# A hybrid decoder layer with 32 streamed experts: gate units among the projections, later MLA norms, other places for output weights and biases

## The chip, the core and the metric

The kernel runs on one core of a Trainium2 chip. TensorE (PE) multiplies matrices, VectorE (DVE) and ScalarE (ACT) do elementwise work, GpSimd (POOL) helps with it, and SyncE (SP) issues the transfers, which run on 16 DMA engines. The metric is device microseconds from the start to the end of one execution; less is better. Three runs of the kernel before took 1162.37, 1165.75 and 1166.36 us, a median of 1165.75.

## What is computed

One decoder layer on 256 tokens of width 1024, in float32. The reference, cut to its frame:

```python
proj = rmsnorm(x, g_mix) @ w_in          # q, k, v | c_q, c_kv, k_pe | gate_a, gate_b
q_a = apply_rope(rmsnorm(q_a, moba_q_norm)); k_a = apply_rope(rmsnorm(k_a, moba_k_norm))
y_a = moba_attention(q_a, k_a, v_a)      # 8 heads of 64; one block of 256: causal softmax
q_b = rmsnorm(c_q, mla_q_lat_norm) @ w_uq;  kv = rmsnorm(c_kv, mla_kv_lat_norm) @ w_ukv
...                                      # norm and rope of q_b, k_b (8 heads of 96)
y_b = causal_attention(q_b, k_b, v_b)
merged = sigmoid(gate_a) * (y_a @ w_branch_a) + sigmoid(gate_b) * (y_b @ w_branch_b)
x = x + merged @ w_out
x = x + routed_experts(rmsnorm(x, g_ffn), ...)   # top 4 of 32, clamped SwiGLU, 1024 wide
x = x + sigmoid(rmsnorm(x, g_ple) @ w_ple_gate) * (p_i @ w_ple_proj)
```

## The kernel before

The program has two parts. The first, up to about 215 us, is all that stands ahead of the experts; the second is a loop, written out, over 32 experts, and a short tail for the last gate.

**Weights of the first part** come as units of 128x1024 float32 (512 KB), in the order of the list `KINDS`: latent projection (a), q, k, the up projections (u), v, 16 gate units (g), 8 branch units (b) and 8 output units (o). `fetch` issues their loads on SyncE into four places `raw` (ring slot 6) and three places `raw_x`; `raw_of` gives the place, and from unit `RAW_LAST` on only the three `raw_x` are used. `make_unit` splits a unit in two fp32r halves: ACT casts the high half (L210), DVE subtracts 5/8 of the low half and GpSimd 3/8 (both L214); for output units DVE subtracts all. `unit` does that up to three units ahead of the one that PE takes. Each product is then three matmuls, high by high, high by low and low by high (`three`, L251 to L253).

**The order** in the first part: latent and q projections, `moba_norm(0)` (norm and rotation of q, with the multiplies by the norm's factor at L358), k projection, `moba_norm(1)`, up projections, v projection, one gate unit, transposes (`moba_T`), `mla_norm` (statistics, the factor chain called hb, rotation, and the multiplies of q by hb at L470), another gate unit. Then eight steps of attention, each with the scores of the next pair of heads, a gate unit, the probabilities' transposes (PT, L550), another gate unit and the values. In `scores` the fixed factor 1/sqrt(d) is applied with the mask (L534). After the attention come the branch products with the merge by gates, and the output projection (wo) in two halves of 512 columns; the router's transposes and logits lie between its units. Engines run their instructions in order; the code's order and the scheduler of the framework set it.

**Expert weights** are pieces of 2 MB, four for gate and up and two for down per expert, listed in `seq`. They go into ten slots: 0 to 7 of the ring, and 8 and 9, which exist once the pool of gates is closed. `release` issues the next piece on SyncE into a slot that has been given free in the program. Ahead of the loop the slots serve other ends and are given up one after another: 7 after the first projection, 3 after the k projection, 6 once unit `RAW_LAST` is made, 5 after the first attention half, 4 after the attention, then 8, 9, and 0 to 2 after the output projection. The gates are kept in three tiles of a pool of their own (`t8`), the three-fold expert biases in the tile `pre8`, which are loaded after the attention and split into bf16 parts (L661 to L667).

**The loop**: gather by a one-hot product (L779), gate and up product (L818), SwiGLU on DVE and ACT, transposes, down product (L842) and scatter into accumulators (L852). At expert 20 stands a branch (`overflow`, L898): if any expert has more than 64 tokens, an inner loop loads its weights again. With these inputs the branch is not taken. `load` issues on SyncE unless another engine is named.

## Time and profile before

| | |
|---|---|
| median of three runs | 1165.75 us |
| the profiled execution | 1165.23 us |
| its span, first to last instruction | 1163.5 us |
| PE busy | 1076.0 us (92%) |
| DVE, ACT, POOL busy | 337.9, 201.4, 78.2 us |
| moved by DMA | 440.18 MB, mean 378 GB/s over the span |

The rows below are numbered in groups. Times are us from the span's start, unless marked ns. A name such as L818 is a line of the kernel; "g<-w_g,xg" says what is written from what. "A <- B" in a list of waits says that A sat idle until B ended. A Q behind an engine's name (SPq, PEq) is its instruction queue. PEclk is the clock that TensorE was granted, as a share of full speed.

### The profile page before, as it was taken

How to read it: one execution, taken by the hardware profiler on the slowest of the kernel's cores; microseconds unless marked ns; L12 is line 12 of the kernel's file. 1: busy time of each engine (PE TensorE's matmuls, PEld its weight loads, DVE VectorE, ACT ScalarE, POOL GpSimd, SP SyncE). 2: the span in 40 equal slices, each digit the busy share in tenths (PEclk: the TensorE clock that was granted, in tenths of full speed). 3: DMA queues.
4: the chain of work that ended last, by engine and by line, in shares of the span. 5: the costliest groups of instructions: out<-in, count | busy, mean ns of one | idle time of the engine just before them, and what ended most of it. 6: DMA issues, size and time to landing. Idle time of an engine off the chain costs nothing. (4 is left out here: it accounts for less than half of the span.)

```text
span 1163.5 us, 13110 instructions
## 1 busy us (share of the span) xinstructions
PE 1076.0 (92%) x5446; PEld 525.8 (45%) x5446; DVE 337.9 (29%) x754; ACT 201.4 (17%) x375; POOL 78.2 (7%) x84
## 2 busy tenths in 40 slices
PE   8889999999999999998889999998899999998988
PEld 6668997543434343343333434333334333333336
DVE  6987686321111122111110111120111111111136
ACT  5547644211000000000001000000000000000024
POOL 5553320000000000000000000000000000000000
PEclk9999999999999999999999999999999999999999
DMA  9653568699999999999999999999899999999991
GB/s 363 221 181 113 184 225 317 274 430 430 429 431 430 431 430 431 429 429 409 432 431 430 430 430 430 431 431 426 347 432 430 430 430 431 430 430 431 427 412 40
DMA packets 39649, 440.18 MB, mean 378 GB/s; under 512 B 4384, under 2 KB 5152, under 8 KB 14144
## 3 DMA queue, kind: packets, MB, share of 16 engines
q1 hardware_dynamic: 39584, 439.27, 90.7%
q8 instruction: 45, 0.74, 0.2%
q14 instruction: 20, 0.16, 0.0%
HBM read 438.21 MB, written 1.05 MB: 378 GB/s over the span
## 5 line engine op out<-in xcount | busy, mean ns | idle before, releaser
L818 PE MATMUL g<-w_g,xg 128*64 128x512 f32 x1024 | 295.4, 597 | 28.3 <-DMA w_g<-in_wgu 24.3
L818 PE MATMUL u<-w_g,xg 128*64 128x512 f32 x1024 | 292.5, 593 | 0.0
L842 PE MATMUL y<-w_d,ht 128*64 128x512 f32 x1024 | 234.5, 596 | 14.5 <-DMA w_d<-in_wdn 12.9
L822 DVE TENSOR_SCALAR g<-g 128x512 f32<-128x512 f32 x32 | 22.1, 691 | 467.2 <-PE g L812 467.2
L818 PEld LDWEIGHTS g<-w_g,xg 128*64 128x64 f32 x1024 | 79.3, 136 | 172.4 <-issue 120.6
L818 PEld LDWEIGHTS u<-w_g,xg 128*64 128x64 f32 x1024 | 83.1, 137 | 144.7 <-issue 141.9
L842 PEld LDWEIGHTS y<-w_d,ht 128*64 128x64 f32 x1024 | 72.8, 136 | 139.4 <-issue 119.3
L824 ACT ACTIVATE th<-g 128x512 f32<-128x512 f32 x32 | 20.2, 630 | 482.9 <-DVE g L822 482.9
L847 DVE COPY ys<-y 64x512 f32<-64x512 f32 x32 | 22.2, 695 | 171.2 <-ACT ys L846 171.1
L852 PE MATMUL acc<-ys,owT 128*128 128x512 f32 x128 | 59.2, 605 | 8.8 <-ACT ys L846 8.8
L846 ACT COPY ys<-y 64x512 f32<-64x512 f32 x32 | 18.5, 579 | 262.0 <-PE y L842 262.0
L852 PEld LDWEIGHTS acc<-ys,owT 128*128 128x128 f32 x128 | 22.9, 189 | 45.7 <-ACT ys L846 21.1
L779 PE MATMUL g<-oh,h_perm 128*128 128x128 f32 x256 | 33.1, 282 | 6.8 <-DVE g L822 5.6
L210 ACT CAST fr<-raw_x 128x1024 fp32r<-128x1024 f32 (+1 forms) x33 | 33.9, 1033 | 21.8 <-PE proj L253 5.6
L214 POOL TENSOR_TENSOR fr<-raw_x,fr 128x384 fp32r<-128x384 f32 (+1 forms) x25 | 34.6, 1389 | 44.9 <-ACT fr L210 37.9
L779 PEld LDWEIGHTS g<-oh,h_perm 128*128 128x128 f32 x256 | 29.9, 191 | 16.9 <-DVE g L822 10.6
L214 DVE TENSOR_TENSOR fr<-raw_x,fr 128x640 fp32r<-128x640 f32 (+2 forms) x33 | 33.0, 1000 | 5.8 <-ACT fr L210 5.6
L779 PEld LDWEIGHTS u<-oh,h_perm 128*128 128x128 f32 x256 | 29.8, 192 | 8.1 <-issue 8.1
L252 PE MATMUL proj<-fr,fr 128*128 128x512 f32 (+1 forms) x64 | 26.0, 406 | 7.1 <-DVE fr L214 6.5
L779 PE MATMUL u<-oh,h_perm 128*128 128x128 f32 x256 | 32.2, 279 | 0.0
L251 PE MATMUL gate<-fr,fr 128*128 128x256 f32 x104 | 31.2, 300 | 0.0
L253 PE MATMUL gate<-fr,fr 128*128 128x256 f32 x104 | 30.1, 290 | 0.0
(316 smaller groups left out, 1124.5 us busy)
## 6 DMA issues: line engine op xcount, KB each, us to landing
w_g<-in_wgu SPq DMA_DIRECT2D x124, 2048.0 KB, 32.1
w_d<-in_wdn SPq DMA_DIRECT2D x62, 2048.0 KB, 32.9
raw_x<-in_wpre SPq DMA_DIRECT2D x38, 512.0 KB, 4.3
w_g<-in_wgu SPq DMA_DIRECT2D x8, 1024.0 KB, 28.6
raw<-in_wpre SPq DMA_DIRECT2D x8, 512.0 KB, 6.2
w_d<-in_wdn SPq DMA_DIRECT2D x4, 1024.0 KB, 24.5
w_ple<-in_w_ple_gate SPq DMA_DIRECT2D x8, 512.0 KB, 14.1
raw<-in_wpre SPq DMA_DIRECT2D x4, 416.0 KB, 7.6
```

Source lines behind the costliest of these rows:

```text
L210: A.copy(hi, src)
L214: e.tensor_tensor(lo[:, a:b], src[:, a:b], hi[:, a:b], op=ALU.subtract)
L251: T.matmul(o, lh, rh, start=first, stop=False)
L252: T.matmul(o, lh, rl, start=False, stop=False)
L253: T.matmul(o, ll, rh, start=False, stop=last)
L779: T.matmul(b[:, k * P:(k + 1) * P], h_perm[:, tt, (half * 4 + k) * P:(half * 4 + k + 1) * P], oh[:, tt], start=(tt == 0), stop=(tt == 1))
L818: T.matmul(gu[i][half * CAP:(half + 1) * CAP], xg[:, k], wv_, start=(k == 0), stop=False)
L822: V.tensor_scalar_min(g, gu[0], 7.0)
L824: A.activation(th, g, AF.Tanh, scale=0.851)
L842: T.matmul(y[g * CAP:(g + 1) * CAP], ht[:, f % 4, (f // 4) * CAP:(f // 4 + 1) * CAP], w[:, dh * 512:(dh + 1) * 512], start=(f == 0), stop= ...
L847: V.tensor_copy(ys[CAP:P, 1 - odd], y[CAP:P])
L852: T.matmul(acc[tt][dh], owT[:, dh, tok(tt)], ys[:, dh], start=first, stop=last)
```

## The change

- `KINDS` puts one gate unit behind each of the q, k and v projections, and the v projection ahead of the up projections; the other 13 gate units follow. The gates are kept in ring slot 3, which no longer takes a piece after the k projection. Four gate units now stand ahead of the first scores, one in each attention step up to the fifth ahead of the transposes, and one behind them in seven steps.
- The factor of q's norm, times 1/sqrt(d), is no longer multiplied into q but given to the exponential as its scale, and to the maximum; that takes away the two multiplies at L358 for q and those at L470. `moba_norm` and the transposes of the latents stand behind the v projection. `mla_norm` is cut in `mla_stats` (behind the second scores) and `mla_norm` (behind the third).
- The first four output units have places of their own in slot 4 after the attention (`raw_o`); slot 4 takes its piece when the fourth is made. Slot 6 takes its piece at unit 24 instead of 18.
- The biases are loaded into slot 3 after the merge, and split in the code where they were; slot 3 takes its piece behind the split. The additional tile for split units is there before the first scores.
- The loads of the overflow loop are issued by GpSimd.

```diff
--- before.py
+++ after.py
@@ -46,14 +46,14 @@
 C_ALL = 1859


-KINDS = (("a", 4, 832), ("q", 4, 1024), ("k", 4, 1024), ("u", 1, 1024), ("u", 1, 512), ("u", 1, 1024), ("v", 4, 1024),
-         ("g", 16, 1024), ("b", 8, 1024), ("o", 8, 1024))
+KINDS = (("a", 4, 832), ("q", 4, 1024), ("g", 1, 1024), ("k", 4, 1024), ("g", 1, 1024), ("v", 4, 1024), ("g", 1, 1024),
+         ("u", 1, 1024), ("u", 1, 512), ("u", 1, 1024), ("g", 13, 1024), ("b", 8, 1024), ("o", 8, 1024))
 UNITS = [(kind, n) for kind, c, n in KINDS for _ in range(c)]
 U_OFF = [sum(n for _, n in UNITS[:i]) for i in range(len(UNITS) + 1)]

-N_RAW, N_EXTRA, RAW_LAST = 4, 3, 18
+N_RAW, N_EXTRA, RAW_LAST = 4, 3, 24
 FIRST_O = len(UNITS) - 8
-LAST_THREE = 27
+LAST_THREE = 25

 WARM0, WARM2, WARM3, WARM5 = 30, 30, 8, 10
 AHEAD = 3
@@ -180,6 +180,8 @@
     made, used, sent_units, holder = [0], [0], [0], {}

     def raw_of(n):
+        if FIRST_O <= n < FIRST_O + N_RAW:
+            return N_RAW + N_EXTRA + n - FIRST_O, raw_o[0][:, n - FIRST_O]
         i = n % (N_RAW + N_EXTRA) if n <= RAW_LAST else N_RAW + n % N_EXTRA
         t = raw[:, i] if i < N_RAW else raw_x[:, i - N_RAW]
         return i, t[:, 0:UNITS[n][1]]
@@ -194,6 +196,8 @@

         while sent_units[0] < limit:
             n = sent_units[0]
+            if n >= FIRST_O and not raw_o:
+                return
             i, t = raw_of(n)
             if holder.get(i, -1) >= made[0]:
                 return
@@ -201,7 +205,7 @@
             load(t, wpre[:, U_OFF[n]:U_OFF[n + 1]])
             sent_units[0] += 1

-    taken = {}
+    taken, raw_o = {}, []

     def make_unit(n):
         src = raw_of(n)[1]
@@ -225,6 +229,8 @@
             made[0] += 1
             if m == RAW_LAST:
                 release(6)
+            if m == FIRST_O + N_RAW - 1:
+                release(4)
             fetch()
         return (split[split_of(n)][:, u, 0:UNITS[n][1]].rearrange("p (k f) -> p k f", k=k) for u in range(2))

...
+    both_gates = slot(3, "sg")
+    sg = [both_gates[:, o:o + 2048].rearrange("p (u t) -> p u t", u=8) for o in (0, 2048)]
+    gi = iter(range(16))
+    def gate_unit():
+        a, ft = divmod(next(gi), 8)
+        b = bank("gate")
+        wh, wl = unit(8)
+        for k in range(8):
+            three([(b[:, :S], (wh[:, k], wl[:, k]), (xh[:, k], xl[:, k]))], k == 0, k == 7)
+        o = sg[a][:, ft, :]
+        V.tensor_tensor(o, b[:, :S], rbc, op=ALU.mult)
+        A.activation(o, o, AF.Tanh, scale=0.5)

     project(512, lambda tt, b: A.mul(qk[:, tt, 0:512], b, xrs[:, tt:tt + 1]))
+    rbw = wk.tile([P, 2, P], F32, name="rbw")
+    rbc = wk.tile([P, S], F32, name="rbc")
+    for tt in range(2):
+        V.tensor_scalar_mul(rbw[:, tt], ones, xrs[:, tt:tt + 1])
+    b = bank("rbc")
+    for tt in range(2):
+        T.matmul(b[:, tok(tt)], rbw[:, tt], ident, start=True, stop=True)
+    V.tensor_copy(rbc, b[:, :S])
+    gate_unit()
+    project(512, lambda tt, b: A.mul(qk[:, tt, 512:1024], b, xrs[:, tt:tt + 1]))

     G.tensor_tensor(w_r, w_r, gkp.unsqueeze(2).broadcast_to([P, 8, NE]), op=ALU.mult)
     kpe = wk.tile([P, 2, 32], F32, name="kpe")
...
+    gate_unit()
+    project(512, lambda tt, b: A.mul(va[:, tt], b, xrs[:, tt:tt + 1]))
...
-    b = bank("rbc")
-    for tt in range(2):
-        T.matmul(b[:, tok(tt)], rbw[:, tt], ident, start=True, stop=True)
-    V.tensor_copy(rbc, b[:, :S])
-    project(512, lambda tt, b: A.mul(qk[:, tt, 512:1024], b, xrs[:, tt:tt + 1]))
-    release(3)
-    moba_norm(1)
+    gate_unit()
+    qscale = [None, None]
...
+        hrs = rsqrt(wk, hss.rearrange("p a b -> p (a b)"), 16, 64, f"ha{i}")
+        if not i:
+            V.tensor_scalar_mul(hrs, hrs, 64.0 ** -0.5)
+            qscale[0] = hrs.rearrange("p (t h) -> p t h", t=2)
...
+            if i:
+                V.tensor_tensor(src, src, hrs[:, tt].unsqueeze(2).broadcast_to([P, 8, 64]), op=ALU.mult)
+    moba_norm(0)
...
-    project(512, lambda tt, b: A.mul(va[:, tt], b, xrs[:, tt:tt + 1]))
+    moba_norm(1)
+    gate_unit()
...
-    def mla_norm():
+    brs = [None]
+    def mla_stats():
...
-        brs = rsqrt(wk, bss.rearrange("p a b -> p (a b)"), 32, 96, "hb")
-        brs = brs.rearrange("p (t h) -> p t h", t=2)
+        r = rsqrt(wk, bss.rearrange("p a b -> p (a b)"), 32, 96, "hb").rearrange("p (t h) -> p t h", t=2)
+        V.tensor_scalar_mul(r[:, :, 0:8], r[:, :, 0:8], 96.0 ** -0.5)
+        qscale[1] = r[:, :, 0:8]
+        brs[0] = r
+    def mla_norm():
...
-            V.tensor_tensor(q4[:, tt], q4[:, tt], brs[:, tt, 0:8].unsqueeze(2).broadcast_to([P, 8, 96]), op=ALU.mult)
-            kr = brs[:, tt, 8:16].unsqueeze(2)
+            kr = brs[0][:, tt, 8:16].unsqueeze(2)
...
-        scale = (96.0 if mla else 64.0) ** -0.5
+        scale = qscale[int(mla)]
...
+                V.tensor_tensor_reduce(pr[:, c0:c1], b[:, c0:c1], mask[:, c0:c1], 1.0, NEG, ALU.add, ALU.max,
                                        mx[:, i:i + 1])
-            V.tensor_scalar_mul(mx[:, 2:4], mx[:, 0:2], -1.0)
+            h = 2 * j + u
+            V.scalar_tensor_tensor(mx[:, 2:4], in0=mx[:, 0:2], scalar=-1.0, in1=scale[:, :, h], op0=ALU.mult, op1=ALU.mult)
...
-                A.activation(pr[:, c0:c1], pr[:, c0:c1], AF.Exp, bias=mx[:, 2 + i:3 + i], accum_out=mx[:, 4 + i:5 + i])
+                A.activation(pr[:, c0:c1], pr[:, c0:c1], AF.Exp, bias=mx[:, 2 + i:3 + i], scale=scale[:, i, h:h + 1],
+                             accum_out=mx[:, 4 + i:5 + i])
...
-    sg.append(t8tile("sga"))
-    gi = iter(range(16))
-    gate_unit(next(gi))
     moba_T()
-    mla_norm()
-    gate_unit(next(gi))
+    split.append(t8tile("split").bitcast(FR))
     Ps = {0: scores(0, False)}
     for j in range(8):
         if j + 1 < 8:
             Ps[j + 1] = scores((j + 1) % 4, j + 1 >= 4)
-        if j < 7:
-            gate_unit(next(gi))
+        if j == 0:
+            mla_stats()
+        if j == 1:
+            mla_norm()
+        if j < 5:
+            gate_unit()
         pts = probs_T(Ps.pop(j))
         if j < 7:
-            gate_unit(next(gi))
+            gate_unit()
         values(j % 4, j >= 4, pts)
         if j == 3:
             release(5)
@@ -587,17 +617,12 @@
             for i in range(2):
                 mla_T(i, 0)
                 mla_T(i, 1)
-            sg.append(t8tile("sgb"))
-            split.append(t8tile("split").bitcast(FR))
     att_stack.close()
-    b96 = h8[0:96]
-    load(b96, bgu3)
     mixed = gate_stack.enter_context(tc.tile_pool(name="mixed", bufs=2, side="right"))
-    release(4)
...
-    sga = sg[0].rearrange("p t (u f) -> p (t u) f", u=4)
-    sgb = sg[1].rearrange("p t (u f) -> p (t u) f", u=4)
+    raw_o.append(slot(4, "raw_o").rearrange("p (n f) -> p n f", n=N_RAW))
...
+    sga, sgb = sg
...
     gate_stack.close()
+    b96 = slot(3, "b96")[0:96, 0:2048]
+    load(b96, bgu3)
...
         V.tensor_copy(bgu[r, c], b96[r, c])
+    release(3)
...
                     for k in range(8):
-                        load(wt, wgu[bass.ds(e, 1), k // 2, :, k % 2 * 2048:k % 2 * 2048 + 2048].rearrange("o p f -> p (o f)"))
+                        load(wt, wgu[bass.ds(e, 1), k // 2, :, k % 2 * 2048:k % 2 * 2048 + 2048].rearrange("o p f -> p (o f)"), G)
                         gate_up_k(gu, xg, k, wt)
...
                     for f in range(8):
-                        load(wt[:, 0:1024], wdn[bass.ds(e, 1), f // 4, :, f % 4 * 1024:f % 4 * 1024 + 1024].rearrange("o p f -> p (o f)"))
+                        load(wt[:, 0:1024], wdn[bass.ds(e, 1), f // 4, :, f % 4 * 1024:f % 4 * 1024 + 1024].rearrange("o p f -> p (o f)"), G)
                         down_k(y, ht, f, wt[:, 0:1024], 0)
...
```

SyncE, the issues around the merge: raw_x and raw_o are units, w_gCE and w_dCE piece C of expert E, b96 and pre8 the biases. Before:

```order
L80 DMA w_g01_1646<-in_wgu 128x4096
L80 DMA raw_x_85<-in_wpre 128x1024 x9
L80 DMA w_g11_1982<-in_wgu 128x4096
L80 DMA raw_x_85<-in_wpre 128x1024
L80 DMA w_g21_2013<-in_wgu 128x4096
L80 DMA w_d10_2105<-in_wdn 128x4096
L80 DMA w_g31_2101<-in_wgu 128x4096
L80 DMA w_d00_2103<-in_wdn 128x4096
```

Now:

```order
L80 DMA raw_x_85<-in_wpre 128x1024 x4
L80 DMA b96_1939<-in_bgu3 96x2048
L80 DMA w_g30_1965<-in_wgu 128x4096
L80 DMA w_g01_1979<-in_wgu 128x4096
L80 DMA raw_x_85<-in_wpre 128x1024
L80 DMA w_g11_2010<-in_wgu 128x4096
L80 DMA w_d00_2102<-in_wdn 128x4096
L80 DMA w_g21_2098<-in_wgu 128x4096
L80 DMA w_g31_2100<-in_wgu 128x4096
L80 DMA w_d10_2131<-in_wdn 128x4096
```

Before, the biases and the pieces g30 and g01 were sent ahead of the merge's end and five pieces behind it; now the biases stand ahead of seven pieces.

DVE around the first scores: L534 and L562 are the masked scores with their maximum, hb_ the factor chain of the MLA norm, L501 and L364 gates, L214 and L218 unit splits. Before:

```order
L501 TENSOR_TENSOR sga<-gate,rbc 128x256
L456 TENSOR_SCALAR bss<-bss,kps 128x8
L214 TENSOR_TENSOR fr_81<-raw_x,fr_81 128x640
L88 TENSOR_SCALAR hb_m<-bss 128x32
L534 ISA pr,mx<-S,mask 128x128
L534 ISA mx 128x1
L90 TENSOR_SCALAR hb_s<-hb_m 128x32
L534 ISA pr,mx<-S,mask 128x256
L534 ISA mx 128x1
L92 TENSOR_SCALAR hb_r<-hb_s 128x32
```

Now:

```order
L218 TENSOR_TENSOR fr_80<-raw,fr_80 128x640
L490 TENSOR_REDUCE bss<-pre_64 128x8
L364 TENSOR_TENSOR sg<-gate,rbc 128x256
L492 TENSOR_REDUCE bss<-kbf 128x8 x2
L494 TENSOR_SCALAR bss<-bss,kps 128x8 x2
L510 TENSOR_TENSOR qb<-qb,pre_64 128x768
L511 TENSOR_TENSOR qb<-qb,rt_778 128x8x32
L490 TENSOR_REDUCE bss<-pre_64 128x8
L562 ISA pr,mx<-S,mask 128x128
L562 ISA mx 128x1
```

The hb chain has left the first scores; split units and gates stand ahead of them in its place.

DVE in the output projection: xs<-wo is a half's residual, 128x1024 from raw_x an output unit's split, bgu and pre8 or b_1939 the biases. Before, from the last bias operations on:

```order
L666 TENSOR_TENSOR pre_64<-pre_64,bgu 32x512
L214 TENSOR_TENSOR fr_81<-raw_x,fr_81 128x1024
L667 CAST bgu<-pre_64 32x512
L214 TENSOR_TENSOR fr_80<-raw_x,fr_80 128x1024
L652 SCALAR_TENSOR_TENSOR xs<-wo,xs 128x512 x2
L214 TENSOR_TENSOR fr_80<-raw_x,fr_80 128x1024
L652 SCALAR_TENSOR_TENSOR xs<-wo,xs 128x512 x2
```

Now, from the first half's residual on, the start and the end of the stretch:

```order
L218 TENSOR_TENSOR fr_80<-raw_x,fr_80 128x1024
L679 SCALAR_TENSOR_TENSOR xs<-wo,xs 128x512 x2
L693 TENSOR_TENSOR b_1939<-b_1939,bgu 32x512
L689 TENSOR_TENSOR b_1939<-b_1939,bgu 96x512
L694 CAST bgu<-b_1939 32x512
L690 CAST bgu<-b_1939 32x512
L692 CAST bgu<-b_1939 32x512
```

```order
L692 CAST bgu<-b_1939 32x512
L693 TENSOR_TENSOR b_1939<-b_1939,bgu 32x512
L694 CAST bgu<-b_1939 32x512
L218 TENSOR_TENSOR fr_80<-raw_x,fr_80 128x1024
L679 SCALAR_TENSOR_TENSOR xs<-wo,xs 128x512 x2
L699 TENSOR_TENSOR fss<-fss 128x2
```

Between the first half's residual and the last unit's split now stand 19 bias operations; before there were none.

## Rows read from the trace of the kernel before

**Rows 1.** Chain of waits: start us, us, what; two pieces before TensorE's tail.

```profile
1046.94 40.00 DMA w_d<-in_wdn
1086.98 3.65 PE y L842 x16
```

**Rows 2.** Timeline of SyncE's queue: start us, us, line; the first issue in the loop.

```profile
222.78 0.33 SPq L80 DMA_DIRECT2D w_g<-in_wgu  x1
```

**Rows 3.** Windows, loop: stretch, us, busy (instructions) by engine, PEclk, DMA share, GB/s.

```profile
215.40:222.80 7.40, 7.40 (x50) 4.83 (x52) 3.72 (x13) 0.00 (x0) 0.00 (x0) 1.00 0.26 113
222.80:816.00 593.20, 565.80 (x2690) 221.85 (x2688) 98.78 (x192) 45.46 (x80) 0.00 (x0) 1.00 1.01 428
816.00:828.00 12.00, 12.00 (x75) 6.82 (x73) 4.13 (x8) 1.56 (x3) 0.00 (x0) 1.00 0.61 233
828.00:1133.00 305.00, 272.55 (x1272) 104.58 (x1268) 47.94 (x85) 24.90 (x40) 0.00 (x0) 1.00 1.01 429
```

**Rows 4.** TensorE's waits: who waits <- for whom: us in total, times, longest.

```profile
PE g L818 <- DMA w_g<-in_wgu: 24.3, 21, 2.3
PE y L842 <- DMA w_d<-in_wdn: 12.9, 17, 1.3
...
PE proj L252 <- DVE fr L214: 6.5, 5, 2.2
...
PE PT L550 <- DVE hb_r L97: 4.8, 2, 4.4
```

**Rows 5.** Timeline of TensorE: a gate unit's first, the next operation, the loop's first.

```profile
71.42 0.28 PE L251 MATMUL gate<-fr,fr 128*128 128x256 f32 x1
...
74.30 0.93 PE L436 MATMUL qkT<-cst,qk 128*128 128x128 f32 x7
...
215.35 2.02 PE L779 MATMUL g<-oh,h_perm 128*128 128x128 f32 x16 [1.20 <-issue]
```

**Rows 6.** Waits of SyncE's queue: the overflow branch.

```profile
SPq L898 <- SPq L898: 29.5, 2, 24.7
```

**Rows 7.** Line L898 on SyncE: ns min/median/max, first and last start us.

```profile
L898 SPq EVENT_SEMAPHORE  x8: 17/17/17, 818.1 to 823.4; - x8
...
L898 SPq COMPARE_BRANCH  x1: 50/50/50, 793.4 to 793.4; - x1
```

**Rows 8.** Windows, DVE's tight stretch: sum of 14:35, 35:50, 50:71, 71:88.

```profile
sum 74.00, PE 62.21 PEld 50.57 DVE 66.25 ACT 39.19 POOL 45.42; mean PE 15.55 PEld 12.64 DVE 16.56 ACT 9.80 POOL 11.35
```

**Rows 9.** DVE by line and form, 0 to 240 us: busy us, mean ns | idle before.

```profile
L214 DVE TENSOR_TENSOR fr<-raw_x,fr 128x640 fp32r<-128x640 f32 x24 | 22.7, 948 | 1.5 <-ACT fr L210 1.3
...
L356 DVE TENSOR_TENSOR qk<-qk,pre 128x512 f32<-128x512 f32 x4 | 5.5, 1366 | 1.4 <-POOL pre L354 1.4
...
L501 DVE TENSOR_TENSOR sga<-gate,rbc 128x256 f32<-128x256 f32 x8 | 3.3, 416 | 1.7 <-PE gate L253 1.7
...
L666 DVE TENSOR_TENSOR pre<-pre,bgu 32x512 f32<-32x512 f32 x4 | 3.3, 813 | 0.1
...
L358 DVE TENSOR_TENSOR qk<-qk,ha_r 128x512 f32<-128x512 f32 x4 | 2.6, 685 | 0.0
...
L470 DVE TENSOR_TENSOR qb<-qb,hb_r 128x768 f32<-128x768 f32 x2 | 1.9, 945 | 0.0
...
L665 DVE CAST bgu<-pre 32x512 bf16<-32x512 f32 x4 | 1.7, 418 | 0.1
```

**Rows 10.** Windows before the loop, columns as in rows 3.

```profile
35.00:50.30 15.30, 13.06 (x51) 9.84 (x51) 14.50 (x31) 3.92 (x6) 7.42 (x8) 0.89 0.44 138
79.00:88.30 9.30, 4.90 (x41) 4.11 (x40) 9.30 (x33) 4.66 (x14) 6.65 (x5) 1.00 0.40 115
88.30:111.40 23.10, 22.73 (x179) 20.42 (x179) 18.88 (x69) 14.90 (x44) 7.76 (x4) 0.93 0.33 95
177.70:205.60 27.90, 26.68 (x122) 21.79 (x121) 16.38 (x26) 10.35 (x16) 0.00 (x0) 0.94 0.85 323
```

**Rows 11.** Page, DMA issues: transfer, queue, count, KB each, us to landing.

```profile
w_g<-in_wgu SPq DMA_DIRECT2D x124, 2048.0 KB, 32.1
```

54 lines of the change are left out of this document (19 added, 35 removed).

## The prediction, made before the result

> **What bounds the kernel now.** I read the chain of waits first. Backwards from the end it is TensorE (PE) for some 76 us, and before 1086.98 it is one expert-weight transfer after another [rows 1]. The windows say the same of the rate: from the first loop transfer at 222.78 [rows 2] to 816 the core moves 428 GB/s and from 828 on 429 GB/s with the DMA share at 1.01, and PE is busy only 565.8 of 593.2 us in the first of these stretches [rows 3]. The list of PE's waits agrees: 24.3 us in 21 waits for gate-up weights and 12.9 us in 17 for down weights [rows 4]. So the loop from 222.8 to 1087 runs at the rate of the weight stream, and PE has 37.2 us to spare in it. Nothing in the change makes the stream itself smaller; only two things can shorten the time: the stream resumes earlier, or it has fewer holes.
>
> Two holes show. From 215.4 to 222.8 the rate is 113 GB/s: all ten slots hold pieces and the next transfer leaves only when the first gate-up piece has been used up [rows 2, 3]. PE begins the loop's first gather at 215.35 [rows 5]; the first slot comes free 7.4 us later. So whatever brings PE to that gather earlier brings the rest of the stream, and with it the end, earlier by as much, as long as the slots are full by then. The second hole is 816 to 828, at 233 GB/s [rows 3]. There SyncE stands 24.7 us in the branch around the overflow loop: the branch is reached at 793.4, and eight semaphore waits follow from 818.1 to 823.4 [rows 6, 7].
>
> **The change, part by part.** The sum is made against the profiled execution's 1165.23 us (span 1163.5 and 1.7 around it); the median of the runs shown is 1165.75, 0.5 us more, which I leave out.
>
> 1. *Overflow loads by GpSimd.* In the branch that is not taken, SyncE's eight waits are for the counts of its own loads in that loop. SyncE issues the weight stream too, so it stands until pieces that it sent before the branch have landed, and sends none meanwhile. With the loads on GpSimd the not-taken side has its waits on GpSimd, which has no loads under way and nothing later to do for SyncE; SyncE goes on after a few branch instructions. Refund: (430 − 233) GB/s × 12 us = 2.36 MB, at 430 GB/s 5.5 us. PE waits 37.2 us for the stream in all, so the refund reaches the end. Ends: 0 if another wait keeps SyncE there, 5.5 if none does; I take 5.5, since the rows name SyncE's own queue as releaser. The additional semaphore waits at the kernel's end cost some tenths; I take 0.
>
> 2. *Projections up to the first probabilities.* Here VectorE (DVE) is the tight engine: 66.25 us busy of the 74 us from 14 to 88, while PE is busy 62.21 [rows 8]. PE waits 6.5 us for weight splits by DVE in the projections, and 4.8 us for the chain of the MLA factor (hb), which stands in the middle of the first scores' softmax [rows 4]. The change drops the multiplies of q by its factor: two at L358, 0.685 each, and two at L470, 0.945 each, together 3.3 us [rows 9]. It puts the hb chain and one of the two rotations of the MLA q behind the first probabilities. By the order that is some dozen operations, most of them smaller than any row here or only trading places with the scores' own; I count four at the 0.42 us of the cheapest row, 1.7 us. It adds two gate units ahead of the first scores (four before the first score matmul instead of two, and one more behind): two splits of 0.95 and two evacuations of 0.42, 2.7 us [rows 9]. DVE then has 66.25 − 3.3 − 1.7 + 2.7 = 64.0 us; at the same share of 0.895 that takes 71.5 us instead of 74: 2.5 us earlier. The other end is PE's: its idle time in the stretch is 74 − 62.2 = 11.8 us, and the two additional units fill 5.8 of it, so at most 6.0 us. I take 3.5, nearer to the DVE end, because DVE was the fuller engine. On top, two more gate units are then done that before came later, and PE is the limit there (busy 22.73 of 23.1 us, then nearly all of it [rows 10]). One unit takes PE 71.42 to 74.30 = 2.88 us [rows 5], so 5.8 us. Together **9.3**, between 8.3 and 11.8 if the order does what it says; less is the first rival.
>
> 3. *Clock.* In the K projection the granted clock is 0.89 over 15.3 us, and after the wait for hb 0.93 over 23.1 us [rows 10]; that is 1.7 + 1.6 us of missing clock, each behind a stretch in which PE waited (79 to 88.3 it was busy 4.9 of 9.3 us). A gate unit between projections gives PE work while DVE splits. I take 1.0; ends 0 and 3.3.
>
> 4. *Output weights, biases.* From 177.7 to 205.6 PE is busy 26.68 of 27.9 us at clock 0.94 [rows 10]: 1.2 idle and 1.7 lost to the clock, 2.9 at most to win. The last output unit waits for its transfer before; now four units have their own places and come earlier. Against it, 19 of the 24 bias operations now stand on DVE between the two halves of the output projection, ahead of the last unit's split (the order below the change). At 0.42 to 0.81 us each [rows 9] that is 8 to 15 us. They start after the first half, about 15 of the 27.9 us into the stage, and PE asks for that unit, the last of eight, some 22 us in. The low end costs PE about 2 us, the high end 9. The higher means come from operations slowed beside GpSimd, which has no instruction in this stage [rows 10], so I take near the low end, and a gain of **1.5** for the whole part from the 2.9 less its share; ends −5 and 2.9.
>
> 5. *Places.* Two weight pieces more than before have to be fetched after the merge, because slots 3 and 4 are lent to gates, output units and biases: 2 × 2.1 MB [rows 11] at 430 GB/s = 9.8 us, less about 1.5 for output units fetched earlier. Idle transfer time there before: 27.9 × (1 − 323/430) = 6.9 us, and 7.4 × (1 − 113/430) = 5.5 us in the hole [rows 3, 10], so 12.4 against 8.3. It fits with some 4 us left. I take 0; the third rival is that it doesn't.
>
> Sum: 5.5 + 9.3 + 1.0 + 1.5 = 17.3 us, 1165.2 − 17.3 = 1147.9, so **1148**. PE's slack of 37.2 us carries it: after the 5.5 some 32 us of waiting for weights are left, and a start moved as a whole takes none of it.
>
> **Rivals.** *A: DVE stays the bound and the projections give little.* For it: DVE operations beside GpSimd are long; the rotation's multiply at L356 takes 1.37 us where L358 with the same 128x512 takes 0.685 [rows 9], and GpSimd's share of each split stays. If the two units only push DVE's work later, part 2 gives nothing beyond 2 to 5 us and part 4 nothing: from 1165.2 − 5.5 = 1159.7 down to 1153.5. Against it: the gate units' PE work has to be done anyway and idle PE time of 11.8 us lies ahead of it. The Trainium skill speaks for it ("SBUF — State Buffer", "Who interferes with whom"): a DVE instruction with two SBUF inputs contends with a GpSimd instruction that reads SBUF. By that rule each unit moved into this stretch puts one more GpSimd subtract beside the rotations; the rows of L356 and L358 agree with it in size.
>
> *B: the loads by GpSimd change nothing.* The hole would stay if SyncE waited there for something other than its own loads: 1165.2 − 11.8 = 1153.4. The Trainium skill ("DMA: Bandwidth & Descriptors", "Issuing engines are not separate DMA queues") says that transfers from any engine end on the same 16 engines and that another issuer saves only issue time. By that rule alone a new issuer would give nothing. The rows show 24.7 us of SyncE waiting, not issuing, so I give it little.
>
> *C, slower: the store is not full when the loop begins.* Seven pieces are sent after the merge, where five were. They leave SyncE in one order, behind one load for biases that needs its slot from the gates, and one output unit's place. If the first leaves as late as the end of the output projection, all seven (14.7 MB, 34 us) land some 62 us after the merge where the first release came 45 us after it (222.8 − 177.7): 17 us of stream lost. With nothing gained in the projections that gives 1165.2 − 5.5 + 17 = 1176.7. It decides from the point where the first piece leaves more than about 6 us after the merge. Against it: the slot of the first piece is empty at the merge's end, and only the queue stands before it.
>
> **How the numbers follow.** Forecast 1148, with 1142 to 1153 as its own range: 0.68. A 0.16 (1153 to 1160), B 0.05, C 0.04, and 0.07 for more than forecast (parts 2 to 4 near their upper ends, down to 1137). The range 1141 to 1156.5 leaves out C, the worse half of A and the best of the last. A measurement can tell about 0.5%, 5.8 us: faster means below 1159.9. The forecast, B, most of A and the better side give 0.90 for that; the worst of A and mild forms of C 0.06 for the same; C 0.04 for slower.
>
> **What would show it.** In the profile of the changed kernel: no wait of SyncE in the overflow branch and 430 GB/s from 816 to 828's counterpart; the first gather of the loop about 12 us earlier, near 203.5; PE's wait for splits in the projections below 6.5 us and none for hb ahead of the first probabilities; the stage of the output projection near 26.4 us; and the rate between first gather and first release still low, as a sign that the slots were full. The prediction is wrong if the first gather is less than 5 us earlier, if PE waits for weights within the first expert, or if the branch still stops SyncE.

## The result and the profile after

Measured on one chip with the kernel before, four runs each: **1156.55 us** (1154.64 to 1156.99) against 1165.42 us (1162.37 to 1166.36). The ratio is 0.9915, 95% interval 0.9894 to 0.9935: a gain of 8.9 us by the medians and 9.9 by the ratio, about half of the 17.3 forecast. The time lies outside the forecast's own 1142 to 1153, among those of rival A, and at the upper edge of the whole range, 1156.5. The profiled execution took 1156.99 us with a span of 1155.3.

I first laid the places side by side that the prediction names, by the start of TensorE's (PE's) first operation in each:

```
us from the span's start              before    after   earlier   predicted
first probabilities transposed (PT)    88.34    93.25    -4.91      +3.5
merge done, output projection begins  177.71   172.43     5.28     +10.3
loop's first gather                   215.35   210.58     4.77     +11.8
first slot released                   222.78   218.01     4.77     +11.8
last wait for a weight piece ends    1086.98  1078.57     8.41     +17.3
```

So in this pair of profiles 4.8 us came from the stages before the loop, where I wanted 11.8, and 3.6 us from inside the loop, where I wanted 5.5. The prediction named three signs of being wrong. One has come: the first gather is less than 5 us earlier. The other two have not: PE waits for no weights within the first expert, and the branch no longer stops SyncE.

Windows of the changed kernel (columns as in [rows 3]): its tight stretch of projections, the 23.1 us behind the first probabilities, the output projection, first gather to first release, and three around the overflow branch.

```profile
71.00:93.00 22.00, 18.13 (x116) 15.71 (x114) 15.04 (x37) 15.63 (x30) 11.79 (x12) 0.92 0.36 133
...
93.20:116.30 23.10, 22.98 (x195) 20.77 (x196) 21.04 (x78) 17.51 (x46) 6.68 (x5) 1.00 0.37 115
...
172.40:200.80 28.40, 25.97 (x123) 21.01 (x122) 22.60 (x38) 8.99 (x15) 0.00 (x0) 0.96 0.87 342
...
210.60:218.00 7.40, 7.40 (x50) 4.86 (x52) 3.75 (x13) 0.00 (x0) 0.00 (x0) 1.00 0.94 403
...
780.00:800.00 20.00, 13.96 (x56) 5.28 (x54) 4.10 (x9) 2.27 (x4) 0.00 (x0) 0.90 1.01 424
800.00:812.00 12.00, 12.00 (x52) 4.19 (x50) 0.00 (x0) 0.00 (x0) 0.00 (x0) 0.89 1.01 429
812.00:830.00 18.00, 18.00 (x104) 8.89 (x102) 5.15 (x9) 1.79 (x3) 0.00 (x0) 1.00 1.01 431
```

The hole of 233 GB/s at the branch [rows 3] is gone. The output projection takes 28.4 us, no shorter than in [rows 10], where 26.4 was forecast. The rate between first gather and first release is 403 GB/s where it was 113 and was to stay low: pieces were still landing there, so the slots were filled only just in time.

PE's waits in the changed kernel (who waits <- for whom: us in total, times, longest), against [rows 4]:

```profile
PE g L846 <- DMA w_g<-in_wgu: 18.0, 17, 2.3
PE y L870 <- DMA w_d<-in_wdn: 10.1, 14, 1.4
...
PE g L846 <- PEq L926: 5.4, 1, 5.4
PE proj L258 <- DVE fr L218: 4.8, 4, 1.9
PE PT L580 <- DVE pr L571: 2.4, 1, 2.4
PE wo L258 <- DVE fr L218: 2.4, 1, 2.4
```

The wait for hb ahead of the probabilities has gone, as predicted, and two new ones of 2.4 us have come: one ahead of the same transposes, and one in the output projection. 28.1 us of waiting for weights remain, so the loop is still bound by the stream.

### The profile page after: what moved, and what is told of

Read it like the earlier page. It is cut to its first block, busy times and chain, and to the rows that moved or that the text cites. A ratio compares the mean times of both kernels' runs of the same rounds, so it can differ in the third digit from the quotient of the medians.

```text
span 1155.3 us, 13098 instructions
## 1 busy us (share of the span) xinstructions
PE 1076.9 (93%) x5446; PEld 525.8 (46%) x5446; DVE 337.2 (29%) x752; ACT 205.3 (18%) x375; POOL 75.1 (7%) x84
## 5 line engine op out<-in xcount | busy, mean ns | idle before, releaser
L218 POOL TENSOR_TENSOR fr<-raw_x,fr 128x384 fp32r<-128x384 f32 (+1 forms) x21 | 27.3, 1305 | 40.6 <-ACT fr L214 39.2
L819 DVE TENSOR_SCALAR ow<-oh,whalf 128x128 f32<-128x128 f32 x64 | 14.0, 282 | 54.6 <-PE owT L832 54.6
L214 ACT CAST fr<-raw_x 128x1024 fp32r<-128x1024 f32 (+1 forms) x25 | 25.9, 1034 | 20.3 <-PE proj L259 6.4
## 6 DMA issues: line engine op xcount, KB each, us to landing
w_d<-in_wdn SPq DMA_DIRECT2D x4, 1024.0 KB, 24.7
```

What stands on the lines that cost most here:

```text
L214: A.copy(hi, src)
L218: e.tensor_tensor(lo[:, a:b], src[:, a:b], hi[:, a:b], op=ALU.subtract)
```

## The experiments

The kernels ran in groups, each beside runs of the kernel before in the same place: 1168.28 us for a_sync, b_pool, a_lat and a_bias, 1165.17 for a_ctrl, a_dep, a_h8 and a_best, 1166.92 for the last four. Times of different groups are therefore compared by their ratios (such a ratio is not quite that of two medians, which for the changed kernel would be 0.9924). The end of the merge, the first gather and the start of the last down matmul are from one profiled execution each. They scatter: the same program profiled twice (after and a_ctrl) differs by 1.5 us at the gather, and b_pool, whose instructions up to there are those of the kernel before, by 2.2 us from it. So a difference of some 2 us between two profiles says nothing.

```
kernel    median us  ratio [95%]              merge done  first gather  last down matmul starts
before                                          177.71        215.35                  1128.34
after      1156.55   0.9915 [0.9894, 0.9935]    172.43        210.58                  1119.93
a_sync     1159.95   0.9928 [0.9905, 0.9951]    172.90        211.85                  1124.68
b_pool     1162.55   0.9959 [0.9945, 0.9973]    176.63        213.16                  1122.30
a_lat      1155.56   0.9890 [0.9867, 0.9913]    170.72        209.60                  1118.82
a_bias     1159.57   0.9928 [0.9907, 0.9949]    174.05        215.24                  1124.35
a_ctrl     1157.70   0.9931 [0.9907, 0.9955]    172.96        212.06                  1121.42
a_dep      1156.83   0.9928 [0.9904, 0.9953]    171.91        210.52                  1119.76
a_h8       1153.99   0.9908 [0.9878, 0.9937]    170.27        205.19                  1114.46
a_best     1151.87   0.9890 [0.9858, 0.9921]    170.77        205.65                  1114.53
a_order    1161.73   0.9955 [0.9932, 0.9979]    177.22        215.57                  1124.61
a_qmul     1157.56   0.9917 [0.9897, 0.9936]    171.61        210.06                  1119.17
a_noown    1154.32   0.9885 [0.9864, 0.9907]    171.84        208.35                  1117.57
a_lath8    1152.14   0.9866 [0.9846, 0.9885]    170.87        206.47                  1115.74
```

Before the loop, then, the 4.8 us of the first pair are the upper end: the profiles with the old start (before, b_pool) have the gather at 213.2 to 215.4, those with the new one (after, a_ctrl, a_sync) at 210.6 to 212.1, a gain of 1.1 to 4.8 us.

**The loop: where did 1.9 of the 5.5 us go?** a_sync is the changed kernel with the overflow loads given back to SyncE; b_pool is the kernel before with that one edit; a_ctrl is the changed kernel again, as it is.

```diff
 a_sync, against the changed kernel (both overflow loads)
-                        ... .rearrange("o p f -> p (o f)"), G)
+                        ... .rearrange("o p f -> p (o f)"))
```

> The changed kernel with one part undone: the loads of the overflow loop are issued by SyncE again. Theory 1 (the 16 DMA engines drift apart, and the pause lines them up again): the hole of 5.5 us of transfer time comes back, but the piece that PE waits for lands only some 3.7 us later, as the last down product came 8.4 us earlier in the changed kernel of which 4.8 were there at the loop's start; time 1156.6 + 3.7 = 1160.3. Its landings should lie apart by about 5 us ahead of expert 20 and by 1.5 to 2 us behind it. Rival 2 (the hole is worth its bytes): 1156.6 + 5.5 = 1162.1. Rival 3 (the loads do nothing, all of the gain is from ahead of the loop): 1156.6.

> The kernel before with only one part of the change: the loads of the overflow loop are issued by GpSimd. Theory 1 (drift): 1165.4 - 3.7 = 1161.7, no hole near 816 to 828, landings 6 to 7 us apart at the end where the kernel before has 3. Rival 2: 1165.4 - 5.5 = 1159.9. Rival 3: 1165.4. With the parts adding up, this gain and the loss of the run with SyncE's loads in the changed kernel are the same.

> The changed kernel as it is, on the same chip as the three runs below, for which it is the measure. Both theories: ratio to the kernel before 0.9915, the loop's gather within 1 us of 210.6, landings 6 to 7 us apart at the end of the loop.

Line L926 in a_sync (ns min/median/max, first and last start us), and the window there:

```profile
L926 SPq EVENT_SEMAPHORE  x8: 17/17/17, 814.3 to 819.6; - x8
...
L926 SPq COMPARE_BRANCH  x1: 50/50/50, 789.8 to 789.8; - x1
```

```profile
812.00:824.00 12.00, 12.00 (x72) 6.08 (x69) 4.06 (x6) 1.21 (x2) 0.00 (x0) 1.00 0.63 242
```

The same line in the changed kernel:

```profile
L926 POOLq EVENT_SEMAPHORE  x4: 17/43/43, 772.1 to 772.4; - x4
...
L926 SPq COMPARE_BRANCH  x1: 50/50/50, 788.7 to 788.7; - x1
L926 PEldq COMPARE_BRANCH  x1: 7574/7574/7574, 790.0 to 790.0; - x1
```

With SyncE as issuer the eight waits and the hole return (242 GB/s); with GpSimd its four waits are over in 0.3 us and SyncE goes straight on. In b_pool there is no hole either:

```profile
816.00:828.00 12.00, 12.00 (x75) 6.66 (x72) 4.97 (x9) 1.79 (x3) 0.00 (x0) 1.00 1.00 427
```

So the mechanism of part 1 holds, and the bytes came back in full: counted by landed bytes, the changed kernel leads the kernel before by 4.8 us from 60 to 300 MB and by 10.3 us from 310 to 430 MB, which is 5.5 more. But PE did not get them in full. The last wait for a weight piece, in timelines of PE (start us, us, operation, [idle before <-releaser]), in a_sync:

```profile
1083.32 3.65 PE L870 MATMUL y<-w_d,ht 128*64 128x512 f32 x16 [0.42 <-DMA w_d<-in_wdn]
```

in b_pool:

```profile
1080.94 3.65 PE L842 MATMUL y<-w_d,ht 128*64 128x512 f32 x16 [0.44 <-DMA w_d<-in_wdn]
```

and in the changed kernel:

```profile
1078.57 3.65 PE L870 MATMUL y<-w_d,ht 128*64 128x512 f32 x16 [0.43 <-DMA w_d<-in_wdn]
```

[rows 1] has the same product of the kernel before, at 1086.98. From it to the start of the last down matmul all four kernels take 41.36 us, so what is won at this wait is won. Less the earlier first gather, the loop itself gave 3.66 − 3.50 = 0.2 us in a_sync, 6.04 − 2.19 = 3.9 in b_pool and 8.41 − 4.77 = 3.6 in the changed kernel, never 5.5. (That b_pool's gather is 2.2 earlier, with nothing changed ahead of it, is the scatter between two profiles.) The same difference between the last two columns of the table, which that scatter does not touch, is 3.6 to 4.1 us in all twelve kernels with GpSimd's loads.

The marks that the 16 parts of each landing leave in the trace show why. For the piece that this product waits for:

```
              first part   8th/9th (median)   last part   spread    PE starts
before          1083.78        1085.04         1086.94      3.16     1086.98
a_sync          1079.98        1081.28         1083.28      3.30     1083.32
b_pool          1073.77        1077.63         1080.89      7.12     1080.94
after           1070.95        1075.28         1078.53      7.58     1078.57
earlier in after  12.83           9.76            8.41
```

PE starts 0.04 us behind the last part. The first part is 12.8 us earlier, the middle one 9.8, the last only 8.4. The 16 DMA engines drift apart while the stream runs without a pause (mean spread of a landing, us, by stretches of 25 us):

```
from us     225   400   500   700   800   825   900  1000  1100
before     1.74  1.89  3.29  4.67  4.87  1.50  1.87  1.95  3.20
a_sync     1.41  1.77  3.27  4.78  4.86  1.68  2.20  2.20  3.23
after      1.54  1.84  3.23  4.70  5.73  5.99  6.20  7.13  7.74
b_pool     1.75  1.77  3.12  4.46  4.58  5.26  5.91  6.01  7.36
```

The pause at the branch let all 16 finish, and the spread fell from 4.9 to 1.5 us: in the kernel before fewer than 16 DMA packets are under way from 817.8 to 826.7 us, and none at all from 822.5 to 824.9. The engines that were ahead stood longest and the last one shortest, so the hole cost more at the mean rate than at the last part. Without it the drift goes on: from 1100 us on the mean spread is 7.4 to 7.9 us in all twelve kernels with GpSimd's loads and 3.2 in the two without. Two other causes fall. The branch on PE is not it: PE waits 3.5 us for it in a_sync as in a_ctrl. The new start is not it either: b_pool has the old one. Why the engines drift was not tried.

The times alone would not have shown this. b_pool's ratio, 0.9959, is 4.8 us, by its interval 3.2 to 6.4: that the loads do nothing is excluded, but 3.7 and 5.5 both fit. a_sync lies 0.4 us below a_ctrl and 1.5 above the changed kernel by the ratios, where 3.7 was expected, and the intervals overlap. That the edit is worth its 3.6 us within the changed kernel rests on the traces.

**The projections: what holds back the first probabilities?** a_order puts the three gate units back behind the projections (their places in the list of units and in the packed weights too); a_lat does the latents' transposes ahead of the V projection; a_dep makes the MLA statistics wait for the first score maximum; a_qmul restores the multiplies of q.

```diff
 a_order
+    for _ in range(4):
+        gate_unit()                 # and the three calls between projections removed
 a_lat
+    for tt in range(2):             # transposes of the latents and their splits
+        ...
     gate_unit()
     project(512, lambda tt, b: A.mul(va[:, tt], b, xrs[:, tt:tt + 1]))
-    for tt in range(2):
-        ...
 a_dep
+        one = wk.tile([P, 1], F32, name="one")
+        V.tensor_scalar(one, first_mx[0][:, 0:1], 0.0, 1.0, op0=ALU.mult, op1=ALU.add)
...
-            A.square(sq[:, 0:768], qb[:, tt, 0:768])
+            A.activation(sq[:, 0:768], qb[:, tt, 0:768], AF.Square, scale=one)
 a_qmul, the MLA pair (the MoBA pair likewise)
-        qscale[1] = r[:, :, 0:8]
+        qscale[1] = ones[:, 0:16].rearrange("p (t h) -> p t h", t=2)
...
+            V.tensor_tensor(q4[:, tt], q4[:, tt], ..., op=ALU.mult)
```

> The changed kernel, the latents' transposes and their evacuation put ahead of the gate unit in front of the V projection instead of behind the V projection. Theory (the V projection's end leaves one gate unit, 2.9 us, for DVE's six evacuation operations, so PE waits twice 0.93 us for them, falls to half clock, and ACT's casts of the next units stand behind copies of that late product while DVE idles 4.3 us): the two waits go, the up projection takes 4.2 us instead of 7.0, the first probabilities' transposes come 2 to 3 us earlier than 93.25, the loop's gather as much earlier than 210.6. The time follows only as far as transfers are ready: in the changed kernel all slots are full less than 1 us before the first is given free, so 1.5 to 2.5 us, 1154 to 1155. Rival (DVE's total is the bound of this stretch): the first transposes stay within 1 us of 93.25 and the time at 1156.

> The changed kernel with the MLA statistics tied to the first scores: the square takes its scale (1.0) from a cell that is computed from the first scores' maximum, so the statistics and the rotation of q can't be put ahead of them on DVE. Theory (6.6 us of statistics and rotation stand on DVE between the first score matmul and the first masked score, though the code has them behind it; PE waits 2.4 us for the probabilities): the wait goes, the first transposes come 2 to 2.5 us earlier than 93.25, the loop's start 1 to 2 us earlier, time 1 to 2 us less than the changed kernel on this chip. Rival (DVE does the same work later and PE waits there instead): the merge's start and the loop's start within 0.5 us, no gain.

> The changed kernel with one part undone: no gate units among the projections; the same four gate units stand in a row behind the up projections, all else is kept. Theory (the units between the projections give PE work while DVE splits): PE's waits for splits in the k and v projections are 4.8 us in the changed kernel and should be 6 to 8 us here, the first transposes 1 to 3 us later than 93, the loop's gather 1 to 2 us later than in the changed kernel on the other chip (212.1), time 0 to 2 us more. Rival (DVE's total sets the end of the stretch wherever the units stand): first transposes and gather within 1 us, same time.

> The changed kernel with one part undone: q is multiplied by its norm's factors again (two operations of 0.69 us for MoBA, two of 0.94 us for MLA, on DVE), and the exponential's scale is 1. Theory (DVE is full in the stretch up to the first probabilities, so what is taken from it comes back): the MoBA pair moves the first transposes 1 to 1.4 us later; the MLA pair now stands behind them, in a stretch where DVE has room, and costs under 0.5 us; gather 1 to 2 us later, time 1 to 2 us more. Rival (DVE waits 7 us for ACT and PE in this stretch, so that two operations more are hidden): no change within 0.5 us.

PE's waits in a_order:

```profile
PE uq L257 <- DVE fr L405: 5.8, 1, 5.8
PE S L551 <- ACT scr L471: 5.5, 1, 5.5
```

Without gates between them the projections run into two waits of over 5 us, PT comes at 98.51 and the gather at 215.57. So the spread of the gates is what earned the gain before the loop: without it the gather comes 3.5 us later than in a_ctrl and 5.0 later than in after, and the time is 2.8 to 4.7 us more by the ratios, though their intervals overlap. The waits stand elsewhere than expected: those for splits in the projections, expected at 6 to 8 us, are 3.9.

What is still in the way shows in VectorE's (DVE's) timeline of the changed kernel:

```profile
70.83 1.81 DVE L408 TENSOR_TENSOR fr<-lat,fr 128x384 fp32r<-128x384 f32 x2
...
77.96 0.83 DVE L218 TENSOR_TENSOR fr<-raw,fr 128x640 fp32r<-128x640 f32 x1 [4.25 <-ACT fr L214]
...
83.10 0.95 DVE L490 TENSOR_REDUCE bss<-pre 128x8 f32<-128x768 f32 x1
...
85.49 2.10 DVE L494 TENSOR_SCALAR bss<-bss,kps 128x8 f32<-128x8 f32 x2
...
88.82 0.95 DVE L490 TENSOR_REDUCE bss<-pre 128x8 f32<-128x768 f32 x1
89.68 0.28 DVE L562 CUSTOM_DVE_ANT_0 pr<-S,mask 128x128 f32<-128x128 f32 x1
```

The latents' splits (L408) end at 72.6, PE begins the up projection on them late, ScalarE (ACT) casts the next unit only behind the copies of its result, and DVE stands still for 4.25 us. Later the statistics (L490 to L494) stand ahead of the first masked score.

In a_lat the two waits of 0.93 us ahead of the up projection are gone and PE waits 2.5 us for a gate's split instead; PT comes at 90.52, 2.7 us earlier than in after, the gather 1.0 earlier than in after and 2.5 than in a_ctrl. This is not shown to be the edit's work: a_h8, whose instructions up to PT stand in the changed kernel's order on all four engines, has PT at 89.91, also without the two waits. a_lat's ratio is the best of these four, but its interval overlaps the changed kernel's.

a_dep took PT to 88.08, 5.2 us earlier than in after and 4.7 than in a_ctrl, the merge's end only 0.5 and 1.0; the gather, at 210.52, is as in after and 1.5 earlier than in a_ctrl. Its waits of PE have a new row:

```profile
PE O L596 <- ACT pt L586: 2.9, 2, 2.5
```

So earlier probabilities by themselves bought nothing that stands clear of the scatter, and the time is a_ctrl's (0.9928 against 0.9931). a_qmul, with the multiplies back, is no slower (0.9917, PT 91.14, gather 210.06), against what was expected: the 3.3 us of DVE work that part 2 dropped were worth nothing measurable.

**The output projection.** a_bias loads and splits the biases as the kernel before did; a_h8 gives two further output units places of their own, in the tile h8 that is idle then; a_noown takes away the four own places of the change.

```diff
 a_bias
     att_stack.close()
+    b96 = h8[0:96]
+    load(b96, bgu3)
...
     gate_stack.close()
-    b96 = slot(3, "b96")[0:96, 0:2048]
-    load(b96, bgu3)
+    release(3)
...
-    release(3)
 a_h8, in raw_of
+        if FIRST_O + N_RAW <= n < FIRST_O + N_RAW + 2:
+            i = n - FIRST_O - N_RAW
+            return 2 * N_RAW + N_EXTRA + i, h8[:, i * 1024:(i + 1) * 1024]
 a_noown
-        if FIRST_O <= n < FIRST_O + N_RAW:
-            return N_RAW + N_EXTRA + n - FIRST_O, raw_o[0][:, n - FIRST_O]
...
-    raw_o.append(slot(4, "raw_o").rearrange("p (n f) -> p n f", n=N_RAW))
+    release(4)
```

> The changed kernel with the biases loaded and split as before (loaded after the attention into the tile pre8, split in the merge), slot 3 given free at the merge's end. Theory (19 bias operations on DVE stand ahead of the last output unit's split, PE waits 2.4 us for it and then runs 6 matmuls at half clock): the wait and the half clock go, the output projection takes 25.3 instead of 28.4 us, and the merge, where DVE is nearly full, becomes up to 1 us longer; the pieces leave up to 5 us earlier, so the hole from 200 to 205 us (165 GB/s) is smaller. Loop start 2 us earlier, time 1153.5 to 1155. Rival (the merge takes on what the output projection loses, DVE 10 us of bias work in a stretch where it is busy 97%): merge 3 us longer, no gain, 1156.5.

> The changed kernel, and output units 5 and 6 have places of their own too (in the tile pre8, which is free after the attention), so that the last unit is loaded before the merge ends and its split stands ahead of the bias operations on DVE. Theory (in the output projection PE waits 2.4 us for the last unit's split, which stands behind 10 us of bias operations, and then runs at half clock): the projection takes 25 to 26 us instead of 28.4, the loop's gather comes 2.5 to 3 us earlier, the last three pieces too, and the time is 2 to 3 us less than the changed kernel's on this chip. Rival (the last unit isn't what holds the stage): 28 us as before, no gain.

> The changed kernel with one part undone: output units have no places of their own, all eight go through the three places raw_x, and slot 4 takes its expert piece right after the attention. Theory (the last units' loads stand on SyncE's queue behind pieces of 2 MB): one piece more lands ahead of the merge's end, but two output units are now sent behind the biases and pieces, ACT waits for them, the output projection takes 1 to 4 us longer than the 28.4 us of the changed kernel, gather as much later, time 1 to 3 us more. Rival (the earlier piece pays for it): the output projection within 1 us and the time the same or 1 us less.

In the changed kernel the bias operations stand ahead of the last unit's split on DVE:

```profile
185.73 0.68 DVE L693 TENSOR_TENSOR b<-b,bgu 32x512 f32<-32x512 f32 x1
...
195.60 0.42 DVE L694 CAST bgu<-b 32x512 bf16<-32x512 f32 x1
196.04 1.22 DVE L218 TENSOR_TENSOR fr<-raw_x,fr 128x1024 fp32r<-128x1024 f32 x1
```

and PE waits for it; from 198.65 on a product of the same shape takes 0.63 instead of 0.39 us:

```profile
197.32 0.50 PE L258 MATMUL wo<-fr,fr 128*128 128x512 f32 x1 [2.43 <-DVE fr L218]
197.66 0.39 PE L259 MATMUL wo<-fr,fr 128*128 128x512 f32 x1
...
198.65 0.63 PE L258 MATMUL wo<-fr,fr 128*128 128x512 f32 x1
```

In a_h8 the same split stands at 183.48, ahead of the bias operations, and the window of its whole output projection has no idle PE and no lost clock:

```profile
183.48 1.22 DVE L221 TENSOR_TENSOR fr<-raw_x,fr 128x1024 fp32r<-128x1024 f32 x1
184.73 0.68 DVE L696 TENSOR_TENSOR b<-b,bgu 32x512 f32<-32x512 f32 x1
```

```profile
170.30:194.90 24.60, 24.60 (x122) 20.22 (x120) 21.65 (x37) 8.21 (x13) 0.00 (x0) 1.00 0.89 336
```

That is 28.4 − 24.6 = 3.8 us in the stage, and the gather is 5.4 us earlier than in the changed kernel; 2.2 of these stand already at the merge (170.27 against 172.43), ahead of anything that the edit touches, so 3.2 are its own. That is clear of the scatter: from the merge's end to the gather the three kernels with these places (a_h8, a_best, a_lath8) take 34.9 to 35.6 us, and after, a_ctrl, a_sync, a_lat, a_dep and a_qmul 38.1 to 39.1. In time a_h8 is below a_ctrl on the same chip by 3.7 us (medians) or 2.7 (ratios); the intervals overlap.

a_bias shows what happens when the biases simply stay. There the last output unit's load waits for its place and leaves SyncE behind three weight pieces. First SyncE's timeline, then ACT's:

```profile
179.03 3.42 SPq L80 DMA_DIRECT2D w_g<-in_wgu  x3
183.94 0.33 SPq L80 DMA_DIRECT2D raw_x<-in_wpre  x1
```

```profile
199.18 1.04 ACT L214 CAST fr<-raw_x 128x1024 fp32r<-128x1024 f32 x1 [4.09 <-DMA raw_x<-in_wpre]
```

A 512 KB load, 3.8 us to landing by the median in the changed kernel, takes 15 us here, the stage 31.3 us where 25.3 was expected, and the gather comes at 215.24. Its ratio, 0.9928, is not clear of the changed kernel's. (The 165 GB/s in its expectation are 193 in the window from 200 to 205 us.) a_noown, expected 1 to 3 us slower, is at least as fast as the changed kernel (0.9885; the two intervals overlap), with a wait in another place:

```profile
PE lg L653 <- ACT raw_x L651: 2.3, 2, 2.0
```

and a stage of 26.6 us at clock 1.00: DVE has the last split at 194.12 there, ahead of its last bias operations. Four places of their own for the first output units brought nothing measurable; two for the units read last, in a_h8, took the wait away.

**Together.** a_best is a_lat, a_dep and a_h8 in one; a_lath8 leaves a_dep out.

> The changed kernel with the three edits together: latents' transposes ahead of the gate unit before the V projection, statistics tied to the first scores, two more own places for output units. If the causes are separate and the stage sums hold: first transposes at 88 to 89, output projection 25.5 us, loop's gather 5 to 6 us earlier than the changed kernel's; the time follows as far as the slots are full, 3.5 to 5.5 us less than the changed kernel on this chip. Rival (transfers limit): gather 5 us earlier, but the rate has no hole left behind the merge and the time gains under 2.5 us.

> The changed kernel with two edits: latents' transposes ahead of the gate unit before the V projection, and own places for output units 5 and 6. It leaves out the tie of the statistics, which moved the first transposes 4.7 us earlier and the loop's start only 1.5. Theory (the tie gains nothing at the loop's start that these two don't): gather at 204.5 to 205.5 as in the run with all three, ratio to the kernel before 0.987 to 0.990. Rival (the tie carries part of it): gather 1 us or more later than 205.7, ratio 0.991.

Both beat the kernel before and, by their medians, the changed kernel: 1152.14 us against 1166.92 (0.9866) for a_lath8, whose interval (0.9846 to 0.9885) lies below the changed kernel's (0.9894 to 0.9935); those of a_best and a_h8 overlap with the latter. a_lath8's gather, 206.47, lies between the 205.5 of its theory and the 206.7 of its rival, so whether the tie adds anything in a_best is open. Which of these three is the fastest can't be told from these runs.

## Why the prediction was right and wrong, step by step

1. **Overflow loads, 5.5 forecast, 3.6 measured.** Who waited, for what, and the bytes that came back were right, and rival B fell: the hole went with the issuer. The Trainium skill ("DMA: Bandwidth & Descriptors", "Issuing engines are not separate DMA queues") lets another issuer save only the time to issue; the trace agrees that the transfers are no faster (429 GB/s behind the branch before [rows 3], 429 to 431 in the windows above), and shows beside it 24.7 us in which the issuer was held [rows 6] and now is not. The step that failed is "PE waits 37.2 us for the stream in all, so the refund reaches the end". It took the mean rate for the arrival of a piece. PE waits for the last of 16 parts, and that part came only 8.4 us earlier where the middle one came 9.8 and the bytes 10.3.

2. **Projections, 9.3 forecast and 10.3 with the clock; 5.3 measured at the merge.** The failing step is "64.0 us; at the same share of 0.895 that takes 71.5 us instead of 74". The rows that answer to [rows 8], the K projection and the sum from 14 to 93 us, are:

```profile
35.00:50.00 15.00, 13.54 (x68) 11.03 (x67) 14.68 (x27) 6.20 (x8) 8.53 (x9) 1.00 0.55 176
...
sum 79.00, PE 68.31 PEld 57.38 DVE 66.85 ACT 44.09 POOL 48.03; mean PE 17.08 PEld 14.35 DVE 16.71 ACT 11.02 POOL 12.01
```

DVE is busy 2.9 us more than I reckoned, at a share of 0.846. One error is in my sum: of the 3.3 us of multiplies that I took out, 1.9 never stood in that stretch. In the kernel before the two at L470 ran behind the first probabilities' transposes at 88.34 (ns min/median/max, first and last start us):

```profile
L470 DVE TENSOR_TENSOR qb<-qb,hb_r x2: 944/945/946, 89.5 to 91.3; 128x768 f32<-128x768 f32 x2
```

Two more terms differ, in the groups of DVE operations from 14 us to the first probabilities (busy us, mean ns | idle before):

```profile
L95 DVE TENSOR_TENSOR lat_t<-lat_r 128x4 f32<-128x4 f32 x3 | 2.1, 689 | 0.1
...
L565 DVE SCALAR_TENSOR_TENSOR mx<-mx,ha_r 128x2 f32<-128x2 f32 x3 | 1.1, 363 | 0.0
```

The first group, the same three operations, took 0.5 us before; but the other two steps of its chain (L96 and L97) took 3.8 us before and 3.0 here, so the chain is 0.8 us longer. The second is the factor's new place in the softmax, which I had not priced; in its place stood 0.5 us (L536). On the other side the hb chain alone took about 3 us in that stretch before, all of it gone, where I counted 1.7 for it and a rotation together. So these terms do not close the sum, and the rest is open. The share fell because DVE itself waited (us in total, times, longest), where it had waited 0.8 us for such casts before:

```profile
DVE fr L218 <- ACT fr L214: 7.6, 4, 4.2
```

So PT came 4.9 us later instead of 3.5 earlier. My other end failed too: it left PE 6.0 us of idle time in the stretch at most, and 10.7 stayed (79.0 − 68.3). What saved half of the gain is that PT was not the gate: from PT to the merge's end PE took 79.2 us instead of 89.4. (a_dep says the same: PT 4.7 us earlier than in a_ctrl, the merge's end 1.0.) Two gates' 5.8 us are the forecast part; 2.3 us less idle PE (78.67 busy of 79.2, before 86.53 of 89.4) and some 1.7 us of clock (0.98 to 1.00) make up most of the rest. The 5.3 us are of one pair of profiles; with b_pool, a_ctrl and a_sync they are 3.7 to 5.3.

3. **Clock, 1.0 forecast.** The two stretches named came back to 1.00: some 1.6 us each, counting [rows 10]. But the wait ahead of the up projection brought 0.92 over 22 us, 1.8 us of new loss, so about 1.5 net. That this is close to the forecast is luck, since the loss was not in it. It is contained in the 5.3 above.

4. **Output weights and biases, 1.5 forecast, −0.5 measured.** The price was right: 10.3 us of bias operations ahead of the last split (8 to 15 estimated), and PE waits 2.4 us for it (about 2 estimated). The step that failed is "the 2.9 less its share". That gain did not come: the wait took the place of the last unit's transfer, and the clock stayed at 0.96. I had the row that decides in the order of DVE, and counted a refund beside a cost that stood in its way. a_h8 has both: 3.8 us. The −0.5 are again of one pair: from the merge's end to the gather before and b_pool take 36.5 to 37.6 us, after, a_ctrl and a_sync 38.1 to 39.1, so the changes of this part cost 0.5 to 2.6 us; a_noown, without the own places, takes 36.5.

5. **Places, 0 forecast.** Right in its effect, wrong in its margin. The gap between first gather and first release was filled at 403 GB/s, so of the 4 us that I reckoned with little was left. It still sufficed in a_h8, where the gather came at 205.19 with 407 GB/s behind it and the last down product ended 5.5 us earlier than in the changed kernel, as much as the gather. How much earlier a gather the store would bear was not tried. Rival C did not occur.

Of the rivals, A (chance 0.16) described the outcome better than my forecast: "DVE stays the bound and the projections give little" gave 1153.5 to 1159.7. It did so partly for another reason, since DVE was not fuller but waited more. That the time came out at the edge of my whole range supports no step of the sum: three of its four terms were too high.

## What to carry to other kernels

When a hole in a stream is closed, price it at the landing of the last part of a piece, not at the mean rate, and look at the spread of the parts before and after the hole. When work is spread to fill an engine's waits, don't keep the old busy share of the engine beside it: list what each of its waits will be for in the new order, and ask whether the point that moves is the gate at all. And a refund and a cost that meet at the same wait are not added: the later of the two is what is left.

## What the hardware showed that I had not expected

The 16 DMA engines that carry one stream drift apart: in the changed kernel the parts of one 2 MB landing lay 1.5 us apart at 225 us and 7.7 us at 1100 us, with the rate at 428 GB/s from 218 to 780 us and 430 from 830 to 1080. The pause at the branch, in which the stream ran dry for 2.4 us, brought them back to 1.5 us. It made no difference whose edits stood around it: all twelve kernels without the pause drift on, before and a_sync both fall back. The Trainium skill ("DMA: Bandwidth & Descriptors", "Two DMAs through the same engine are not ordered") says that nothing orders DMAs across the 16 engines, and the trace agrees: landings follow each other every 4.9 us, and at a spread of 7.6 us the first part of one (1070.95) comes ahead of the last part of the one before (1073.67).

The branch around the overflow loop, not taken, cost PE's queue 5.9 us in the kernel before, in a_sync and in a_ctrl, 6.3 in b_pool and 7.6 in the changed kernel's first profile, where the other engines took 0.05 to 0.07 us. PE waits 3.5 to 5.4 us for it, inside the slack of the stream. What it consists of, and why two profiles of the same program differ by 1.7 us, was not tried.
